# First weights in four pieces on ScalarE's queue, a later statistic, DeltaNet's side work one unit on, and norm spreads as rounded products

## The chip, the cores and the metric

The kernel runs on one core of one Trainium2 chip. The metric is the device time of one execution in microseconds, the median of several runs; the time before is 1535.09 us (three runs: 1535.09, 1535.09 and 1531.98).

## What is computed

A decoder trunk of two layers over 512 positions of width 1024, in float32:

```python
for layer in range(2):
    j = layer // 2
    if layer % 2 == 0:
        h = h + gated_deltanet(rms_norm(h, dn_norm[j]), ...)   # 8 heads of 128, chunked delta rule
    else:
        h = h + conformer_conv(rms_norm(h, cv_norm[j]), ...)   # GLU, causal conv of width 31, LayerNorm
    h = h + memory_cross_attention(rms_norm(h, xa_norm[layer]), rms_norm(mem, xa_mem_norm[layer]), ...)
    h = h + sq_relu_mlp(rms_norm(h, mlp_norm[layer]), ...)     # 1024 -> 4096 -> 1024
return rms_norm(h, final_norm)

def rms_norm(x, g):
    return x * lax.rsqrt(jnp.mean(x * x, axis=-1, keepdims=True) + 1e-6) * g
```

Gated DeltaNet projects h to q, k, v, z and to 16 gate columns (b and a per head), runs a causal convolution of width 4 over q, k and v, applies SiLU and a normalisation to q and k, and then carries a 128 x 128 state per head from chunk to chunk, with a decay made from the a column and a strength beta made from the b column.

## The kernel before

Activations lie transposed: a tile is 128 channels by 512 positions, and x is eight such tiles. Weights come from HBM as 128 x 1024 tiles of 512 KB ("units" of weights: one output tile of 128 channels with its eight blocks of 128 input channels). Every product is made of three rounded ones: a float32 operand is split into a rounded high part (fp32r) and the rounded rest, and high x high, low x high and high x low are summed in PSUM (`mm3`, lines 229 to 231). ScalarE casts the high part of a weight tile (`wh`, line 207), VectorE subtracts to get the low part (`wl`, line 70 by way of `wsplit`). Three weight tiles of each kind are in flight (NW = 3), three raw ones.

The RMS norm is not applied to the input of a projection. `Norm.parts` makes xh and xl of gain x h for each of the eight tiles (lines 297 and 73), and the projection of them is scaled behind the product by the reciprocal root of each position. That number is made by `Norm.stat`: the squares are summed over the eight tiles, four small products with a column of ones (ssq, line 315) sum over the channels, ScalarE takes the root, VectorE the reciprocal, and VectorE multiplies the identity with it into a diagonal `dg`. `Norm.spread` multiplies a 128 x 128 matrix of ones with dg in full float32 (line 325), which repeats the number over all 128 partitions, and ScalarE copies that to `rb`. There are six such norms (n0 of the DeltaNet, then the first attention, the first MLP, the conformer, the second attention and the second MLP); the memory has a spread of the same kind over 256 columns (`mem_diag`, `mem_spread`).

The DeltaNet stage is written as a list of main steps on TensorE (`mains`) and a table of side steps (`S.at(unit, rank, ...)`). `run` issues main step i and then the side steps of unit i. A unit of the q, k and v projections is half a head, 12 matmuls; z and the memory's K and V have units of 12 or 24. Unit 0 is `mm_ab`: head 0 of k together with the 16 gate columns (psum `ab`), 40 matmuls; units 1 to 3 have no main step. The constants at the end of the file place the side steps: T_STAT the statistic (the spread two units on, the gates three), T_DEC the decay (its sums `ct` two units before), K2 and Q2 the products among k and q, FS the forward substitution, MG the merging of its blocks, REC the recurrence of each group of four heads, ONORM the norm of its output, HO the transposes into the output projection (`ogT`), TAPV the convolution of v. The tile framework then orders the instructions of each engine from this list; what the order is can be read from the built program. `tc.keep_in_program_order` pins an instruction to its place in the list.

`gates` needs rb: it scales the gate columns, transposes them (abT, line 356), and makes beta, the log decay g and its repeated form `grep` in some twenty small VectorE operations. `decay_sums` multiplies grep (ct, line 419).

At the start SP's queue issues prm, wab (the gate columns' weights), raw0 (the first weight tile, one DMA) and the eight x tiles. TensorE first runs WARM = 13 products of ones.

Of the kernel before, what the change touches and what calls it, by code (L numbers as in the profile page):

```python
# [38 lines left out]
def tile_trunk(ctx, tc, xT, memT, prm_d, adt_d, bdw_d, tap_d, fin_d, w_ab, w_kq, w_v, w_z, w_dno, w_pw1, w_pw2,  # L39
               w_q, w_k, w_vv, w_o, w_up, w_dn, yT):  # L40
    nc = tc.nc
    pe, act, dve, pool = nc.tensor, nc.scalar, nc.vector, nc.gpsimd

    cp = ctx.enter_context(tc.tile_pool(name="cp", bufs=1))
    wp = ctx.enter_context(tc.tile_pool(name="wp", bufs=2))
    fsp = ctx.enter_context(tc.tile_pool(name="fsp", bufs=3))
    up = ctx.enter_context(tc.tile_pool(name="up", bufs=NSLOT))
    sp = ctx.enter_context(tc.tile_pool(name="sp", bufs=13))
# [8 lines left out]
    def slot(dt=F32, s="u", shape=(P, NT)):  # L57
        return up.tile(list(shape), dt, tag="u", name=nm(s))
# [10 lines left out]
    def tt(e, o, a, b, op):  # L69
        return e.tensor_tensor(out=o, in0=a, in1=b, op=op)  # L70

    def stt(o, a, s, b, op0, op1):
        dve.scalar_tensor_tensor(out=o, in0=a, scalar=s, in1=b, op0=op0, op1=op1)  # L73

    def ts(e, o, a, s1, op0, s2=None, op1=None):
        if op1 is None:
# [15 lines left out]
    def pc(name, i=0):  # L92
        return prm[:, OFF[name] + i:OFF[name] + i + 1]

    def load_x():
        r = []
        for t in range(KT):
            h = slot(s="x")
            nc.sync.dma_start(out=h, in_=xT[t * P:(t + 1) * P, :])
# [7 lines left out]
    nc.sync.dma_start(out=raw0, in_=w_kq[0][:, 0:1024])  # L107
# [19 lines left out]
    later = const([P, P], "later", F32R)  # L127
# [38 lines left out]
    for kind, gq in DN_ORDER:  # L166
        for i in range(2):
            j = gq * 2 + i
# [58 lines left out]
    def mm3(ps, wk, xk, first, last):  # L227
        (wh, wl), (xh, xl) = wk, xk
        pe.matmul(ps, wh, xh, start=first, stop=False)  # L229
        pe.matmul(ps, wh, xl, start=False, stop=False)  # L230
        pe.matmul(ps, wl, xh, start=False, stop=last)  # L231

    def wk(w, k):
        c = slice(k * P, (k + 1) * P)
        return w[0][:, c], w[1][:, c]
# [45 lines left out]
    class Sides(dict):  # L281
        def at(self, i, rank, f, *a):
            self.setdefault((i, rank), []).append(lambda: f(*a))


    class Norm:
        def __init__(self, gname, eng=None, deng=None):
            self.eng, self.deng = eng or pool, deng or dve
# [6 lines left out]
        def parts(self, t, h):  # L295
            xh = slot(F32R, "xh")
            act.activation(xh, h, AF.Copy, scale=pc(self.g, t))  # L297
            xl = slot(F32R, "xl")
            stt(xl, h, pc(self.g, t), xh.bitcast(F32), ALU.mult, ALU.subtract)
            self.xs.append((xh, xl))  # L300

        def square(self, h):
# [8 lines left out]
        def stat(self):  # L311
            ps = psum("ssq")
            for c in range(4):
                cs = slice(c * P, (c + 1) * P)
                pe.matmul(ps[:, c:c + 1], self.acc[:, cs], ones[:, 0:1], start=True, stop=True)
# [3 lines left out]
            dve.reciprocal(self.tok, sd)  # L319
            self.dg = slot(s="dg")  # L320
            tt(self.deng, c4(self.dg), over_c(ident), over_i(self.tok), ALU.mult)

        def spread(self):
            ps2 = psum("rb")
            pe.matmul(ps2, ones, self.dg, start=True, stop=True)
            self.rb = slot(s="rb")
            act.copy(self.rb, ps2)

# [439 lines left out]
            del mem[k]  # L768

    def mem_diag():  # L770
        mem["dg"] = slot(s="mdg")
        tt(dve, mem["dg"][:, 0:256].rearrange("p (t j) -> p t j", t=2), over_c(ident, 2), over_i(mem["tok"]), ALU.mult)

    def mem_spread():
        ps = psum("mrs")
        pe.matmul(ps[:, 0:256], ones, mem.pop("dg")[:, 0:256], start=True, stop=True)
        mem["rs"] = slot(s="mrs")
        act.copy(mem["rs"][:, 0:256], ps[:, 0:256])

# [485 lines left out]
    S.at(0, 3, wsplit)  # L1265
    S.at(0, 2, squares, SQ0, 8)
    S.at(T_STAT, 0, n0.stat)
    S.at(T_STAT + 2, 0, n0.spread)
    for h in range(8):
        uk = max(at["k", h] + 1, T_STAT + 2)  # L1270
# [7 lines left out]
    S.at(T_STAT + 3, 1, D.decay_const, 0)  # L1278
# [151 lines left out]
DEC1 = (37, 43)  # L1430
K2 = (14, 13, 16, 17, 43, 44, 47, 46)
Q2 = (16, 18, 20, 21, 46, 48, 48, 51)
FS = ((20, 9), (50, 8))
MG = (34, 67)
V2 = (8, 8)
MGAIN = 12
ONORM = (72, 87)
HO = 76
REC = (42, 74)
MEM = 50  # L1440
MSQ = 14
TAPV = (35, 36, 37, 38, 68, 68, 69, 70)
# [104 lines left out]
```

## Time and profile before

| | us |
|---|---|
| median of three runs | 1535.09 |
| the profiled execution's own time | 1534.16 |
| its span, first to last instruction | 1532.4 |
| TensorE busy | 1514.5 |
| VectorE busy | 895.2 |
| ScalarE busy | 678.8 |
| GpSimd busy | 221.6 |
| mean granted clock | 0.996 |

The profile is of one execution. Its page gives the busy time of each engine, and a line such as `PE ... x512 | 200.2, 391` means 512 instructions, 200.2 us busy together, 391 ns one. Matmuls overlap: one that is listed with 0.39 us follows the one before by 0.23, so what a matmul costs is read from the distance of starts. A product in full float32 appears as two instructions (x2). In a list of waits, `PE S L682 <- DVE vnd L70: 1.2, 1, 1.2` says that TensorE's product into S, line 682, waited for VectorE's vnd, 1.2 us in all, once, 1.2 us at most. In a timeline the columns are start, duration, engine, line, operation, result and operands, count; the brackets hold idle time before and what ended it.

### The profile page before, as it was taken

To read this page: it belongs to the slowest core of one execution; us is meant where nothing else is said; L and a number is where in the kernel's file an instruction comes from. 1 tells how busy PE (TensorE), PEld (TensorE's weight loads), DVE (VectorE), ACT (ScalarE), POOL (GpSimd) and SP (SyncE) were. 2 spreads that over 40 slices of the span, in tenths; PEclk is the share of its full clock that TensorE was granted. 3 is DMA by queue.
4 is the path that set the end of the run, shared out by engine and by line. 5 is a ranking of instruction groups with operands and counts; after the bars stand their busy time and mean duration, and the time that the engine had idled before them with its cause. 6 is when DMAs were issued, how large, how long until landed. Compare 5 with 4: busy or idle time off the path is not lost.

```text
span 1532.4 us, 19347 instructions
## 1 busy us (share of the span) xinstructions
PE 1514.5 (99%) x7560; PEld 1275.3 (83%) x7560; DVE 895.2 (58%) x1342; ACT 678.8 (44%) x1093; POOL 221.6 (14%) x231
## 2 busy tenths in 40 slices
PE   9999999999999999999999999999999999999998
PEld 7888888988888888888888889888888888888886
DVE  6898888766545443443445599774554543434441
ACT  6847655655434442332324564464444441323332
POOL 1321220103112000000002486411111000000000
PEclk9999999999999999999999999999999999999999
DMA  5321123342213222222224524442212222222231
GB/s 178 98 81 65 60 79 111 124 147 87 70 42 110 85 100 98 98 98 100 97 94 162 170 91 142 140 132 92 76 46 96 96 96 97 96 98 97 99 106 55
DMA packets 49051, 153.56 MB, mean 100 GB/s; under 512 B 6208, under 2 KB 8000, under 8 KB 48960
## 3 DMA queue, kind: packets, MB, share of 16 engines
q1 hardware_dynamic: 48960, 152.33, 29.8%
q8 instruction: 59, 0.97, 0.3%
q14 instruction: 32, 0.26, 0.1%
HBM read 149.42 MB, written 2.10 MB: 99 GB/s over the span
## 4 chain that ended last, share of the span: by engine, by line
PE 73%; DVE 5%; DMA 1%; SPq 1%; issue 1%; ACT 1%; POOL 0%; ACTq 0%; DVEq 0%
PE up L231 8%; PE up L229 8%; PE up L230 8%; PE dn L231 7%; PE dn L230 7%; PE dn L229 7%; DVE ca L73 3%; PE q L229 2%; PE xo L230 2%; PE q L231 2%; PE q L230 2%; PE xo L231 2%; PE xo L229 2%; PE pw L230 2%; PE pw L229 2%; PE pw L231 2%
## 5 line engine op out<-in xcount | busy, mean ns | idle before, releaser
L207 ACT CAST wh<-raw 128x1024 fp32r<-128x1024 f32 x248 | 259.9, 1050 | 627.7 <-PE dn L230 194.8
L70 DVE TENSOR_TENSOR wl<-raw,wh 128x1024 fp32r<-128x1024 f32 x231 | 286.3, 1241 | 110.4 <-ACT wh L207 109.2
L229 PE MATMUL up<-xh,wh 128*128 128x512 f32 x512 | 200.2, 391 | 0.0
L231 PE MATMUL up<-xh,wl 128*128 128x512 f32 x512 | 199.2, 389 | 0.0
L230 PE MATMUL up<-xl,wh 128*128 128x512 f32 x512 | 199.2, 389 | 0.0
L231 PE MATMUL dn<-uh,wl 128*128 128x512 f32 x448 | 174.3, 389 | 0.0
L229 PE MATMUL dn<-uh,wh 128*128 128x512 f32 x448 | 174.3, 389 | 0.0
L230 PE MATMUL dn<-ul,wh 128*128 128x512 f32 x448 | 174.3, 389 | 0.0
L70 DVE TENSOR_TENSOR h<-dn,h 128x512 f32<-128x512 f32 x56 | 41.8, 747 | 165.3 <-PE dn L231 165.3
L73 DVE SCALAR_TENSOR_TENSOR rl<-up,rb 128x512 f32<-128x512 f32 x64 | 44.2, 691 | 156.9 <-PE up L231 156.9
L70 POOL TENSOR_TENSOR sq<-sq,sq 128x512 f32<-128x512 f32 x30 | 48.3, 1610 | 469.2 <-ACT sq L304 469.2
L230 PEld LDWEIGHTS up<-xl,wh 128*128 128x128 f32 x512 | 96.1, 188 | 20.5 <-issue 0.5
L229 PEld LDWEIGHTS up<-xh,wh 128*128 128x128 f32 x512 | 96.1, 188 | 20.2 <-issue 0.5
L231 PEld LDWEIGHTS up<-xh,wl 128*128 128x128 f32 x512 | 96.1, 188 | 20.0
L230 PEld LDWEIGHTS dn<-ul,wh 128*128 128x128 f32 x448 | 84.1, 188 | 17.6
L229 PEld LDWEIGHTS dn<-uh,wh 128*128 128x128 f32 x448 | 84.1, 188 | 17.5
L231 PEld LDWEIGHTS dn<-uh,wl 128*128 128x128 f32 x448 | 84.1, 188 | 17.2
L73 DVE SCALAR_TENSOR_TENSOR ca<-x,prm,ca 128x512 f32<-128x512 f32 x112 | 82.3, 753 | 3.5 <-ACT ca L1070 1.3
L229 PE MATMUL h<-xh,wh 128*128 128x512 f32 x192 | 77.5, 404 | 1.4 <-ACT xh L297 1.4
L230 PE MATMUL h<-xl,wh 128*128 128x512 f32 x192 | 75.4, 393 | 0.6 <-DVE xl L73 0.6
L231 PE MATMUL h<-xh,wl 128*128 128x512 f32 x192 | 75.4, 393 | 0.0
L73 DVE SCALAR_TENSOR_TENSOR cva<-cv,prm,cva 128x512 f32<-128x512 f32 x60 | 49.4, 840 | 11.7 <-POOL cva L70 10.4
(346 smaller groups left out, 3065.1 us busy)
## 6 DMA issues: line engine op xcount, KB each, us to landing
raw<-w_up SPq DMA_DIRECT2D x64, 512.0 KB, 3.5
raw<-w_dn SPq DMA_DIRECT2D x64, 512.0 KB, 3.5
raw<-w_pw SPq DMA_DIRECT2D x24, 512.0 KB, 3.6
raw<-w_kq SPq DMA_DIRECT2D x16, 512.0 KB, 3.8
raw<-w_k SPq DMA_DIRECT2D x16, 512.0 KB, 4.1
raw<-w_vv SPq DMA_DIRECT2D x16, 512.0 KB, 3.6
raw<-w_q SPq DMA_DIRECT2D x16, 512.0 KB, 3.6
raw<-w_o SPq DMA_DIRECT2D x16, 512.0 KB, 3.6
```

What stands on the lines that cost most here:

```text
L70: return e.tensor_tensor(out=o, in0=a, in1=b, op=op)
L73: dve.scalar_tensor_tensor(out=o, in0=a, scalar=s, in1=b, op0=op0, op1=op1)
L207: ins = [act.copy(h, raw)]
L229: pe.matmul(ps, wh, xh, start=first, stop=False)
L230: pe.matmul(ps, wh, xl, start=False, stop=False)
L231: pe.matmul(ps, wl, xh, start=False, stop=last)
```

## The change

Four things at once. (1) The first weight tile is loaded by four DMAs of 256 columns issued from ScalarE's queue; on SP wab follows the first x. Casts and subtractions of the quarters and of the x tiles are pinned in the order in which the inputs arrive, two x for each quarter, with the gate weights' cast behind x 0. The second weight tile is split right behind them, ahead of the squares. `mm_ab` takes its products in the order high x high, low weight x high, gates, high weight x low, gates. (2) T_STAT goes from 2 to 5; the spread follows one unit later instead of two and the gates two units later instead of three, so that they stand at units 6 and 7 where they stood at 4 and 5. T_DEC and all other places of DeltaNet's side steps go up by one (MGAIN, MEM and MSQ stay). (3) All norms but n0 and the memory's norm split the reciprocal root into a rounded part and the rest, make two diagonals, and spread them by two rounded products; the matrix `later`, used up to then by the decay, is overwritten with ones for that. (4) WARM goes from 13 to 11.

```diff
-    def load_x():
+    def load_x(then=None):
...
             r.append(h)
+            if then and t == 0:
+                then()
...
     nc.sync.dma_start(out=prm[:, 0:NVEC], in_=prm_d[:, 0:NVEC])
+    raw0 = wp.tile([P, 1024], F32, tag="raw", name="raw0", bufs=NRAW)
+    for i in range(4):
+        act.dma_start(out=raw0[:, i * 256:(i + 1) * 256], in_=w_kq[0][:, i * 256:(i + 1) * 256])
     wab = slot(s="wab")[:, 0:P]
-    nc.sync.dma_start(out=wab, in_=w_ab)
-    raw0 = wp.tile([P, 1024], F32, tag="raw", name="raw0", bufs=NRAW)
-    nc.sync.dma_start(out=raw0, in_=w_kq[0][:, 0:1024])
-    xin = load_x()
+    xin = load_x(lambda: nc.sync.dma_start(out=wab, in_=w_ab))
...
+    def diag2(v, n):
+        vh = sp.tile([P, n], F32R, tag="sm", name=nm("vh"))
+        dve.tensor_copy(vh, v)
+        vl = small(n, "vl")
+        tt(dve, vl, v, vh.bitcast(F32), ALU.subtract)
+        r = []
+        for x in (vh.bitcast(F32), vl):
+            d = slot(F32R, "dg")[:, 0:n * P]
+            tt(dve, d.rearrange("p (c i) -> p c i", c=n), over_c(ident, n), over_i(x), ALU.mult)
+            r.append(d)
+        return r
+
+    def spread2(ps, dg):
+        for i in range(2):
+            pe.matmul(ps, later, dg[i], start=i == 0, stop=i == 1)
...
-            pe.matmul(ps2, ones, self.dg, start=True, stop=True)
+            if self.two:
+                spread2(ps2, self.dg)
+            else:
+                pe.matmul(ps2, ones, self.dg, start=True, stop=True)
...
     def mem_diag():
-        mem["dg"] = slot(s="mdg")
-        tt(dve, mem["dg"][:, 0:256].rearrange("p (t j) -> p t j", t=2), over_c(ident, 2), over_i(mem["tok"]), ALU.mult)
+        act.copy(later, ones)
+        mem["dg"] = diag2(mem["tok"], 2)
...
-    act.copy(ab3[:, :, 0:16], wab.rearrange("p (k x) -> p k x", k=KT))
-    tt(dve, ab3[:, :, 16:32], wab.rearrange("p (k x) -> p k x", k=KT), ab3[:, :, 0:16].bitcast(F32), ALU.subtract)
+    n0 = Norm("dn_norm", dve, False)
...
+    for i in range(4):
+        s = slice(i * 256, (i + 1) * 256)
+        pin(act.copy(hl0[0][:, s], raw0[:, s]))
+        pin(tt(dve, hl0[1][:, s], raw0[:, s], hl0[0][:, s].bitcast(F32), ALU.subtract))
+        for k in (2 * i, 2 * i + 1):
+            n0.parts(k, xin[k], pin)
+            if k == 0:
+                wab3 = wab.rearrange("p (k x) -> p k x", k=KT)
+                pin(act.copy(ab3[:, :, 0:16], wab3))
+                pin(tt(dve, ab3[:, :, 16:32], wab3, ab3[:, :, 0:16].bitcast(F32), ALU.subtract))
     wsplit()
-    n0 = Norm("dn_norm", eng=dve)
-    for t in range(KT):
-        n0.parts(t, xin[t])
...
-            mm3(D.ps["k", 0], wk(w, k), n0.xs[k], k == 0, k == KT - 1)
-            xh, xl = n0.xs[k]
+            (xh, xl), (wh, wl), ps = n0.xs[k], wk(w, k), D.ps["k", 0]
+            pe.matmul(ps, wh, xh, start=k == 0, stop=False)
+            pe.matmul(ps, wl, xh, start=False, stop=False)
             pe.matmul(D.ps["ab"][0:32, :], abp[:, 32 * k:32 * k + 32], xh, start=k == 0, stop=False)
+            pe.matmul(ps, wh, xl, start=False, stop=k == KT - 1)
...
-    S.at(T_STAT + 2, 0, n0.spread)
+    S.at(T_STAT + 1, 0, n0.spread)
...
-    S.at(T_STAT + 3, 0, D.gates)
+    S.at(T_STAT + 2, 0, D.gates)
...
-WARM = 13
+WARM = 11
...
-T_STAT = 2
-T_DEC = 12
+T_STAT = 5
+T_DEC = 13
...
-K2 = (14, 13, 16, 17, 43, 44, 47, 46)
+K2 = (15, 14, 17, 18, 44, 45, 48, 47)
...
-REC = (42, 74)
+REC = (43, 75)
...
```

More of the change, by code (lines that the diff above doesn't have):

```diff
@@ L72, in stt @@
     def stt(o, a, s, b, op0, op1):
-        dve.scalar_tensor_tensor(out=o, in0=a, scalar=s, in1=b, op0=op0, op1=op1)
+        return dve.scalar_tensor_tensor(out=o, in0=a, scalar=s, in1=b, op0=op0, op1=op1)
     def ts(e, o, a, s1, op0, s2=None, op1=None):
@@ L283, in at, with __init__ @@
             self.setdefault((i, rank), []).append(lambda: f(*a))
+    def diag2(v, n):
[12 more added lines that the diff above has]
+            pe.matmul(ps, later, dg[i], start=i == 0, stop=i == 1)
     class Norm:
[L287 to L288 removed]
+        def __init__(self, gname, eng=None, two=True):
+            self.eng, self.two = eng or pool, two
             self.g, self.acc, self.xs, self.n = gname, None, [], 0
@@ L293, in add, with parts @@
             self.square(h)
-        def parts(self, t, h):
+        def parts(self, t, h, pin=lambda i: i):
             xh = slot(F32R, "xh")
-            act.activation(xh, h, AF.Copy, scale=pc(self.g, t))
+            pin(act.activation(xh, h, AF.Copy, scale=pc(self.g, t)))
             xl = slot(F32R, "xl")
-            stt(xl, h, pc(self.g, t), xh.bitcast(F32), ALU.mult, ALU.subtract)
+            pin(stt(xl, h, pc(self.g, t), xh.bitcast(F32), ALU.mult, ALU.subtract))
             self.xs.append((xh, xl))
@@ L314, in stat @@
                 cs = slice(c * P, (c + 1) * P)
-                pe.matmul(ps[:, c:c + 1], self.acc[:, cs], ones[:, 0:1], start=True, stop=True)
+                ins = pe.matmul(ps[:, c:c + 1], self.acc[:, cs], ones[:, 0:1], start=True, stop=True)
+                if not self.two:
+                    tc.keep_in_program_order(ins)
             sd = small(4, "sd")
@@ L319, in stat @@
             dve.reciprocal(self.tok, sd)
+            if self.two:
+                self.dg = diag2(self.tok, 4)
+                return
             self.dg = slot(s="dg")
-            tt(self.deng, c4(self.dg), over_c(ident), over_i(self.tok), ALU.mult)
+            tt(dve, c4(self.dg), over_c(ident), over_i(self.tok), ALU.mult)
         def spread(self):
             ps2 = psum("rb")
-            pe.matmul(ps2, ones, self.dg, start=True, stop=True)
+            if self.two:
+                spread2(ps2, self.dg)
+            else:
+                pe.matmul(ps2, ones, self.dg, start=True, stop=True)
             self.rb = slot(s="rb")
@@ L770, in mem_diag @@
     def mem_diag():
-        mem["dg"] = slot(s="mdg")
-        tt(dve, mem["dg"][:, 0:256].rearrange("p (t j) -> p t j", t=2), over_c(ident, 2), over_i(mem["tok"]), ALU.mult)
+        act.copy(later, ones)
+        mem["dg"] = diag2(mem["tok"], 2)
     def mem_spread():
         ps = psum("mrs")
-        pe.matmul(ps[:, 0:256], ones, mem.pop("dg")[:, 0:256], start=True, stop=True)
+        spread2(ps[:, 0:256], mem.pop("dg"))
         mem["rs"] = slot(s="mrs")
```

24 lines of the change are left out of this document (14 added, 10 removed).

## The prediction, made before the changed kernel ran

> **What bounds the kernel now.** I read the page's shares first, then the list of TensorE's waits, then the timelines of the few places that the change touches.
>
> ```profile
> PE 1514.5 (99%) x7560; PEld 1275.3 (83%) x7560; DVE 895.2 (58%) x1342; ACT 678.8 (44%) x1093; POOL 221.6 (14%) x231
> ...
> L70 DVE TENSOR_TENSOR wl<-raw,wh 128x1024 fp32r<-128x1024 f32 x231 | 286.3, 1241 | 110.4 <-ACT wh L207 109.2
> ```
>
> ```profile
> PE K L231 <- DVE wl L70: 3.3, 2, 2.9
> PE vn L669 <- ACT cvq L459: 1.6, 1, 1.6
> PE h L229 <- ACT xh L297: 1.4, 1, 1.4
> PE S L682 <- DVE vnd L70: 1.2, 1, 1.2
> ...
> PE ai L506 <- ACT cva L466: 0.5, 1, 0.5
> PE dt L441 <- DVE L L73: 0.4, 1, 0.4
> PE vn L669 <- DVE r L73: 0.3, 1, 0.3
> ```
>
> TensorE (PE) is the bound from end to end: it is busy for 99% of the span, and its waits come to some 12 us in all. So time is gained in three ways only: matmul work taken out, waits taken out, or a slow clock avoided; and any new wait of PE is paid in full. The profiled execution took 1534.16 us, its span 1532.4, so 1.8 us lie around the span. The three runs have a median of 1535.09, 0.9 above it. Sums are made against 1534.16.
>
> The start shows all three:
>
> ```profile
> 0.80 1.28 ACT L126 ACT_TABLE_LOAD   x1 [0.80 <-PEq L1538]
> ...
> 1.20 5.85 PE L118 MATMUL warm<-ones 128*128 128x128 f32 x26 [1.20 <-POOL ones L115]
> ...
> 1.71 0.43 SPq L107 DMA_DIRECT2D raw<-w_kq  x1
> ...
> 2.09 0.30 ACT L126 CAST ident_r<-ident 128x128 fp32r<-128x128 f32 x1
> 2.18 4.90 SPq L99 DMA_DIRECT2D x<-xT  x8
> ...
> 6.76 1.04 ACT L207 CAST wh<-raw 128x1024 fp32r<-128x1024 f32 x1 [3.39 <-DMA raw<-w_kq]
> 7.71 5.17 ACT L297 ACTIVATE xh<-x,prm 128x512 fp32r<-128x512 f32 x8
> 8.48 0.49 PE L229 MATMUL h<-xh,wh 128*128 128x512 f32 x1 [1.43 <-ACT xh L297]
> 8.98 5.38 DVE L73 SCALAR_TENSOR_TENSOR xl<-x,prm,xh 128x512 fp32r<-128x512 f32 x8
> 20.21 0.95 PE L315 MATMUL ssq<-ones,sq 128*128 128x1 f32 x8
> ```
>
> The next rows are those of the busy time by stretch: stretch, its length, PE busy (count), PEld, DVE, ACT, POOL, granted clock, DMA share, GB/s.
>
> ```profile
> 6.85:10.26 3.41, 1.41 (x6) 0.61 (x5) 2.43 (x3) 3.41 (x6) 0.00 (x0) 1.00 1.05 403
> 10.26:13.67 3.41, 3.41 (x10) 2.24 (x8) 3.41 (x7) 3.41 (x7) 0.00 (x0) 0.50 1.02 348
> 13.67:17.08 3.41, 3.41 (x16) 2.25 (x16) 3.10 (x6) 3.41 (x8) 0.00 (x0) 1.00 0.49 198
> ...
> 979.60:986.40 6.80, 5.90 (x27) 5.90 (x28) 4.59 (x6) 1.02 (x2) 0.00 (x0) 0.50 0.68 233
> ```
>
> The thirteen warm-up matmuls end at 7.05, the weights land at 6.76, the first real matmul starts at 8.48. PE is then busy for 1.41 of 3.41 us, and the next 3.41 us are granted half the clock: 10 matmuls instead of 16, so 6 x 0.23 = 1.4 us lost. The same happens after the longest wait at 977. The first forty matmuls (head 0 and the gate columns) end where the statistic begins, at 20.21.
>
> **The change part by part.** *Start.* The first weights leave SP's queue for ScalarE's, as four DMAs of 128 KB; on SP x 0 is now second and wab third. ScalarE issues four times at SP's 0.47 each (1.71 to 2.18), from 0.80 to 2.7; behind them stand its table load and the ident_r cast (1.28 + 0.30, to 4.3), then the first quarter's cast. How early x 0 lands no row shows. In these rows the landing of x and of wab is given from the issue:
>
> ```profile
> x<-xT SPq DMA_DIRECT2D x8, 256.0 KB, 5.7
> ...
> wab<-w_ab SPq DMA_DIRECT2D x1, 64.0 KB, 1.8
> ```
>
> From below: second in its queue as wab is now, one issue (0.47) after SP's first at 0.80, 1.27 + 1.8, and 0.65 us for 256 KB at the 403 GB/s of the stretch from 6.85: 3.7. From above: as late as now, where its cast starts at 7.71: 7.5. With all four quarters (512 KB, 1.3 us) ahead of it: 5.0. I take 5.0, because only one DMA stands before it on its own queue. Its cast takes 0.71 (by 8.48 less 7.71, with the hand-over), so xh 0 is there at 5.7, and the warm-up decides: eleven at 0.45 (5.85/13) end at 1.20 + 4.95 = 6.15. PE starts at 6.2 (8.2 at worst). SP's remaining issues wait, in the built program, for the eighth transfer before them over both queues; x 2 thus waits for the first quarter, x 4 for the second, and the next weights for x 2 as they do now.
>
> From there PE must be fed. A pair of x with its quarter costs ScalarE 2 x 0.65 + 0.41 = 1.7 us (0.41 lies on the line from 0.30 at 128 columns to 1.04 at 1024), VectorE 2 x 0.67 + 0.42 = 1.8; PE needs 10 x 0.23 = 2.3 for them. So PE is the slower one and runs on: 0.65 us at half clock (1.5 matmuls), 38.5 x 0.23 = 8.9, about 0.4 for the first subtract and the gate cast: end at 16.1 against 20.21, **-4.1** (from -4.5 to -0.3). The second head's weights follow x 7 on SP's queue with prm's rest (134 + 512 KB, 1.6 us at 403 GB/s); x 7 is cast at 12.2 now (7.71 + 7 x 0.65), so they land by 14 at the latest. Their cast (1.04) now stands before the squares, and with the subtract of 1.24 they are ready near 16.4, when PE's third product there needs them (16.1 + 0.5). Eight squares behind it, at the casts' 0.65 or less, end by 20.3, the sums by 21.0, ahead of the statistic at 21.6, which now has 24 more matmuls before it.
>
> *Gates.* The statistic moves three units on, the spread two, the gates two, but the decay only one. In the built program the gates' transposes are followed by 48 matmuls up to the decay sums (ct), now 60:
>
> ```profile
> 27.68 0.43 PE L356 MATMUL abT<-ident,ab 32*128 32x32 f32 x4
> 33.83 0.69 DVE L70 TENSOR_TENSOR cv<-h,rb 128x512 f32<-128x512 f32 x1 [1.78 <-PE h L231]
> 34.43 0.17 DVE L77 TENSOR_SCALAR sm<-sm 128x32 f32<-128x32 f32 x1
> 38.38 0.19 DVE L73 SCALAR_TENSOR_TENSOR sm<-sm,sm 128x32 f32<-128x32 f32 x1
> 39.13 0.16 DVE L396 COPY grep<-g 128x128 f32<-128x128 f32 x1
> 41.79 0.38 PE L419 MATMUL ct<-tri_mid,grep 128*128 128x128 f32 x2
> ```
>
> Now grep is done 2.5 us before ct. After, VectorE's queue holds the eviction of the last of those 48 (cv of q 0) in front of the last six gate operations. ct stands right behind that head on PE, so PE must wait for one eviction, 0.60 (33.83 to 34.43), and for 38.38 to 39.29, 0.91, with 0.15 of hand-over: **+1.65**. The gate work before it fills VectorE until about the same moment, so up to 1 more. The transposes wait for two evictions put before the gate product: **+0.3**. Behind ct seven matmuls instead of four stand before the dt product that waits 0.4 now: **-0.4**.
>
> *Spreads.* Five norms (not the first) and the memory's spread two rounded products instead of one in full precision:
>
> ```profile
> 835.81 0.23 PE dn L231
> ...
> 854.66 0.86 PE rb L325 x2
> ```
>
> ```profile
> 850.55 0.69 DVE L70 TENSOR_TENSOR dg<-ident,rstd 128x512 f32<-128x512 f32 x1
> ```
>
> 0.86 - 2 x 0.23 = 0.40 each, five times 2.0, and half that for the memory's 256 columns: **-2.2**. VectorE does a copy, a subtract (0.17 each by the row at 34.43) and a second 0.69 more, 1.05 per norm; dg is ready at 851.2 and used at 854.66, so 2.4 us of cover remain. Without that cover it would be the 1.05 each.
>
> *One unit on.* All of DeltaNet's side work keeps its distances but stands one unit (12 matmuls, 2.7 us) later against the projections. Neither order nor trace gives the waits of the two recurrences; they are 1.6, 1.2, 0.5 and 0.3 now. In the built order the second recurrence's state product (1.2) has 24 V matmuls before it where 12 of the out projection stood, so it loses most of its wait; the first one's vn keeps 12 matmuls and nearly the same VectorE queue. I take **-1.0**; bounds are all four gone, -3.6, and each of the four longer by the whole unit of 2.7 (+10.8). At the end of the recurrence the unit is missing:
>
> ```profile
> 341.40 0.89 PE o L699 x8
> ...
> 353.03 1.91 PE L732 MATMUL ogT<-ident,z 128*128 128x128 f32 x16
> ```
>
> ```profile
> 345.67 0.24 DVE L723 RECIPROCAL sm<-sm 128x16 f32<-128x16 f32 x1
> ...
> 345.99 3.54 POOL L70 TENSOR_TENSOR z<-z,sm 128x512 f32<-128x512 f32 x3 [53.30 <-DVE sm L723]
> 347.56 1.06 ACT L207 CAST wh<-raw 128x1024 fp32r<-128x1024 f32 x1 [2.07 <-PE do L230]
> ```
>
> The last o ends at 342.3, ogT runs 48 matmuls later. After, 36 (8.2 us) are left, and ScalarE's root stands behind a weight cast that waits for the first 12 of them (2.75) and takes 1.06; VectorE's reciprocal stands behind that cast's subtract (1.24). Reciprocal near 5.1 + 0.24 and GpSimd's 3.54: 8.95 after o, against 8.2: **+0.9** with what follows (0 to 2).
>
> Sum: -4.1 + 1.65 + 0.3 - 0.4 - 2.2 - 1.0 + 0.9 = -4.85, hence 1529.3. The wait at 977 and its half clock stay: the conformer's queues keep their order.
>
> **The rivals.** *(B) The quarters bring nothing*, because all transfers run at the same 400 GB/s already (403 in the stretch 6.85:10.26) and x 0 waits in the crowd. For it: an x lands 5.7 us after its issue. Against: wab's 1.8, and 512 KB stood before x 0 on one queue. PE then starts at 8.2, the clock drops as now, the start gains 0.3 instead of 4.1: 1533.1. The Trainium skill says just this ("DMA: Bandwidth & Descriptors", section "Issuing engines are not separate DMA queues"): several issuers save the time of issuing alone. By that rule only the place in the queue can help.
>
> *(C) The clock.* PE starts early, yet one stretch of 3.41 us more is granted half clock, because the shorter warm-up or the crumbs of waits among the first products leave a stretch too idle (1.41 of 3.41 was). It costs 1.4: 1530.7. The Trainium skill ("TensorE: Matmul & The Clock Gate", Part 1, the HAM clock gate) has the window free-running, not restarted by a kernel; by that rule the place of the stretches changes from run to run, and 1.4 may come or go in either kernel.
>
> *(D) Slower.* VectorE, busy 184 of 210 us between 30 and 240,
>
> ```profile
> 30.00:240.00 210.00, 207.59 (x1190) 178.05 (x1189) 184.45 (x380) 131.64 (x237) 47.60 (x94) 1.00 0.24 78
> ```
>
> cannot give the unit back: what ct shows (a queue entry tied to a later head) is repeated at the four waits of the recurrences, each time for the whole unit: +10.8 in place of -1.0, 1541.1. It decides once these waits exceed today's by 3.85 us (the sum without its -1.0). Against it: the waits now are only 3.6 in that stage, and the distances among the moved pieces stay.
>
> *(E) All four waits vanish*, 2.6 more: 1526.7.
>
> **How the numbers follow.** Forecast (A) 0.57, C 0.14, B 0.13, D 0.08, E 0.08. About 0.2% (3 us) is what a measurement can tell from no change; against the median that is below 1532.0 for faster and above 1538.2 for slower. A, C and E lie below (0.79); A's own range of 1526.5 to 1532.5 passes that edge, so I give 0.75; same has B and what A and C lose, 0.17; slower is D, 0.08. The range 1525.3 to 1533.4 holds A, C, E and B, and leaves out D.
>
> **What would show it.** First matmul at 6.2 and the statistic's column sums at about 21.6 behind 24 extra matmuls (gain at the end of the forty: 4.1); granted clock 1.00 from about 7 on; a wait of ct on grep of 1.6; spreads of 0.46; ogT waiting 0.7 for GpSimd's z; the list of waits without S. I am wrong if x 0 lands after 5.4, if PE's stretch before 14 is granted 0.50, or if the recurrences' waits add up to more than 3.6.

## The result, and the profile after

| | before | after |
|---|---|---|
| median | 1532.38 (7 runs, 1530.72 to 1535.09) | 1537.72 (7 runs, 1536.53 to 1540.29) |
| ratio, 95% interval | | 1.0033 (1.0023 to 1.0043) |
| profiled execution's span | 1532.4 | 1535.9 |
| TensorE busy | 1514.5 | 1512.7 |

The three runs of before that stand at the head of this document are the first of the seven here. The change made the kernel 5.3 us slower by the medians, where 4.85 less were forecast. The forecast started from one execution of 1534.16, 1.8 above the median of the seven; that moves its time, but not its difference. One run of e13 below took 2162.69 us, and every other run of this document lies within 0.5% of the median of its kernel.

The start did what it should. The list of TensorE's waits of the changed kernel shows where the time went; its columns are the sum, the number of times and the longest, in us.

```profile
PE K L233 <- DVE wl L70: 4.9, 2, 2.6
PE mg L620 <- ACT w L610: 1.8, 1, 1.8
PE ct L446 <- DVE grep L423: 1.7, 1, 1.7
PE vt L648 <- ACT cva L493: 1.7, 1, 1.7
PE vn L696 <- DVE r L73: 1.7, 1, 1.7
...
PE dt L468 <- DVE L L73: 1.1, 1, 1.1
...
PE S L709 <- DVE vnd L70: 0.4, 1, 0.4
...
PE ogT L759 <- POOL z L70: 0.3, 1, 0.3
...
PE abT L383 <- DVE ab L70: 0.2, 1, 0.2
PE rb L352 <- DVE dg L70: 0.2, 1, 0.2
```

`mg`, which never waited before, waits 1.8 us; `vt` waits 1.7 in the first half of the heads, where it did not wait (its 0.3 of before was in the second half), `dt` 1.1 instead of 0.4; of K's 4.9, 2.3 belong to the memory's K inside DeltaNet (0.4 before). `vn` waits as long as before, but for another tile (r, on VectorE, instead of cvq, on ScalarE). S fell from 1.2 to 0.4, `ct` has the 1.7 that was forecast. All waits together are 17.3 us instead of 12.1; with 1.8 us less of busy time that is, to 0.1, the 3.5 us by which the span of the profiled execution grew. The start and two places in the stage, as rows of TensorE's timeline and of the busy time by stretch (columns as in the prediction):

```profile
5.67 0.50 PE L1277 MATMUL h<-xh,wh 128*128 128x512 f32 x1 [0.34 <-ACT xh L316]
...
21.37 0.83 PE L334 MATMUL ssq<-ones,sq 128*128 128x1 f32 x6
```

```profile
4.19:7.60 3.41, 2.82 (x16) 1.89 (x16) 1.75 (x4) 2.43 (x7) 1.37 (x3) 1.00 1.06 374
...
79.30:82.70 3.40, 3.32 (x23) 2.73 (x23) 3.15 (x9) 3.30 (x7) 1.25 (x5) 1.00 0.40 148
82.70:86.10 3.40, 3.40 (x10) 2.66 (x9) 1.90 (x3) 3.30 (x7) 1.17 (x4) 0.50 0.25 81
205.60:209.00 3.40, 3.25 (x28) 2.86 (x26) 3.31 (x11) 2.06 (x5) 1.56 (x4) 1.00 0.45 159
209.00:212.40 3.40, 3.40 (x9) 2.71 (x9) 3.14 (x7) 1.72 (x3) 1.62 (x3) 0.50 0.30 77
```

The first real matmul starts at 5.67 (8.48 before), the granted clock is 1.00 from 4.19, and with 24 matmuls (5.5 us) between the forty and the sums at 21.37 the forty end at 15.9: 4.3 us sooner. Behind that TensorE gives the lead back. The two last pairs of rows are two new stretches of 3.4 us that ran at half clock, which costs at most 1.7 us each; but over all runs the mean granted clock is 0.997 in both kernels, so on average they only stand for the stretches at 10.26 and 979 that went or became shorter.

What the list of waits does not show is the reason for `mg`. These are ScalarE's rows of before between 40 and 65 us, table loads and the decay's exponentials (`egd`, `dt`) alone:

```profile
42.49 1.28 ACT L466 ACT_TABLE_LOAD   x1
...
49.32 1.28 ACT L437 ACT_TABLE_LOAD   x1
50.62 0.25 ACT L437 ACTIVATE egd<-gsum 128x96 f32<-128x96 f32 x1
...
52.01 2.22 ACT L443 ACTIVATE dt<-dt 128x512 f32<-128x512 f32 x4
...
54.74 1.28 ACT L466 ACT_TABLE_LOAD   x1
```

and those of after:

```profile
45.91 1.28 ACT L493 ACT_TABLE_LOAD   x1
...
50.55 1.28 ACT L464 ACT_TABLE_LOAD   x1
51.84 0.25 ACT L464 ACTIVATE egd<-gsum 128x96 f32<-128x96 f32 x1
52.11 1.28 ACT L493 ACT_TABLE_LOAD   x1
...
54.05 1.28 ACT L470 ACT_TABLE_LOAD   x1
55.35 1.08 ACT L470 ACTIVATE dt<-dt 128x512 f32<-128x512 f32 x2
...
58.48 1.09 ACT L470 ACTIVATE dt<-dt 128x512 f32<-128x512 f32 x2
...
61.51 1.28 ACT L493 ACT_TABLE_LOAD   x1
```

L466 (now L493) is the silu of k and q. Before, one silu phase ends, all exponentials run, the next silu phase begins. After, a silu stands between `egd` and the first `dt`: ScalarE loads its table twice more, 2.6 us. Between 20 and 130 us it loads 10 times instead of 8. From 130 to 370 it loads 7 times instead of 9, so that the number for the whole stage is 17 in both kernels: what hurts is where the two loads stand. Behind `dt` hangs the longest chain of the stage: decay blocks, their transpose (FT), 31 dependent rounds of substitution on VectorE, the transpose of their result (TB), then `w` on ScalarE and `mg` on TensorE. In VectorE's rows FT and TB are

```profile
81.20 1.23 DVE L540 STREAM_TRANSPOSE FT<-DB 128x1024 f32<-128x1024 f32 x1
...
114.92 2.11 DVE L556 STREAM_TRANSPOSE TB<-X 128x1024 f32<-128x1024 f32 x1
```

before, and after

```profile
86.16 1.25 DVE L567 STREAM_TRANSPOSE FT<-DB 128x1024 f32<-128x1024 f32 x1 [1.44 <-ACT DB L560]
...
122.58 2.11 DVE L583 STREAM_TRANSPOSE TB<-X 128x1024 f32<-128x1024 f32 x1
```

VectorE, with 31 rounds ahead of it, waits for ScalarE, and TB comes 7.7 us later. One unit is 2.7, and the projections had come 4.3 sooner. The delay grows along the chain: `egd` is 1.2 later, the first `dt` 3.3, FT 5.0, TB 7.7.

### The profile page after: what moved, and what is told of

Same layout as the page of the kernel before. It is cut to its first block, busy times and chain, and to the rows that moved or that the text cites. A ratio compares the mean times of both kernels' runs of the same rounds, so it can differ in the third digit from the quotient of the medians.

```text
span 1535.9 us, 19365 instructions
## 1 busy us (share of the span) xinstructions
PE 1512.7 (98%) x7556; PEld 1273.1 (83%) x7556; DVE 897.9 (58%) x1363; ACT 677.5 (44%) x1097; POOL 221.5 (14%) x231
## 4 chain that ended last, share of the span: by engine, by line
PE 69%; DVE 6%; ACT 1%; issue 1%; POOL 0%; ACTq 0%; DVEq 0%; POOLq 0%
PE up L231 8%; PE up L232 8%; PE up L233 8%; PE dn L232 7%; PE dn L231 7%; PE dn L233 7%; DVE ca L73 4%; PE q L231 2%; PE xo L232 2%; PE xo L233 2%; PE q L233 2%; PE q L232 2%; PE xo L231 2%; PE pw L232 2%; PE pw L231 2%; PE pw L233 2%
## 5 line engine op out<-in xcount | busy, mean ns | idle before, releaser
L70 DVE TENSOR_TENSOR wl<-raw,wh 128x1024 fp32r<-128x1024 f32 (+1 forms) x234 | 287.6, 1231 | 106.7 <-ACT wh L209 100.5
L70 DVE TENSOR_TENSOR h<-dn,h 128x512 f32<-128x512 f32 x56 | 41.8, 747 | 165.3 <-PE dn L233 165.3
L70 POOL TENSOR_TENSOR sq<-sq,sq 128x512 f32<-128x512 f32 x30 | 48.3, 1610 | 464.3 <-ACT sq L323 454.5
L231 PE MATMUL h<-xh,wh 128*128 128x512 f32 x184 | 73.3, 398 | 0.0
L232 PE MATMUL h<-xl,wh 128*128 128x512 f32 x184 | 72.1, 392 | 0.0
L233 PE MATMUL h<-xh,wl 128*128 128x512 f32 x184 | 71.8, 390 | 0.0
L73 DVE SCALAR_TENSOR_TENSOR cva<-cv,prm,cva 128x512 f32<-128x512 f32 x60 | 46.2, 795 | 11.0 <-POOL cva L70 10.5
```

The source lines that it names most:

```text
L73: return dve.scalar_tensor_tensor(out=o, in0=a, scalar=s, in1=b, op0=op0, op1=op1)
```

## The experiments

Medians are in us; runs of one group share their runs of before. First each part of the change alone, or alone undone.

**e1, the spreads alone.** The new spreads in the kernel before.

> The kernel before, with only the five norm spreads and the memory's spread in two rounded products. Theory T1 (the unit by which DeltaNet's side work stands later makes VectorE and ScalarE late for TensorE, and that alone lost the time) and theory T2 (the late statistic lost it) both expect the forecast's term: -2.2 us (ratio 0.9986), each spread 2 x 0.23 instead of 0.86, no new wait of TensorE on dg. Theory T3 (the spreads themselves cost time, by VectorE's extra 1.05 us per norm) expects 0 to +3 us, with a wait of rb on dg.

1531.37 on 1533.29 (the median of this kernel on that of before), ratio 0.9986 (95% interval 0.9977 to 0.9995): -1.9. The forecast's -2.2 holds for this part by itself.

**e2, the unit alone.**

```diff
-T_DEC = 12
+T_DEC = 13
...
-REC = (42, 74)
+REC = (43, 75)
```

> The kernel before, with only the constants that put DeltaNet's decay, transposes, recurrences and output norm one unit later; start, statistic and spreads as before. T1: slower by 5 to 9 us (ratio 1.003 to 1.006), with new waits at mg, at cva before vt, and longer ones of a wl product in DeltaNet, as the changed kernel has. T2: within 2 us of before, since the statistic is early and the distances among the moved pieces stay. T4 (only the two stretches at half clock, at 82.7 and 209, lost the time, and they come by chance): within 2 us, and such stretches at other places or none.

1539.11 on 1533.29, 1.0044 (1.0030 to 1.0057): +5.8 by the medians, 6.7 by the ratio. Waits: vt 2.5, vn 1.5, S 1.6, K's wl product at 267 2.0; TB at 120.4; 10 table loads. (The profile is that of the slowest of the five runs, 1544.48.) So the unit costs by itself what had been forecast as a gain of 1.0.

**e3, the unit undone.** The changed kernel with the unit's constants as before; T_STAT and WARM stay changed.

> The changed kernel with those constants put back to the kernel before; the early start, the late statistic (three units on) and the new spreads stay. T1: the loss in DeltaNet goes but for ct and dt, so -4.3 (start) -2.2 (spreads) +2.5 (ct, dt, abT) = 4 us faster than before (ratio 0.9974). T2: as slow as the changed kernel or slower, 3 to 8 us above before (ratio 1.002 to 1.005), because the decay now stands one unit nearer to the late gates: ct waits 1.7 + 2.7 = 4.4 us.

1534.83, 1.0010 (1.0001 to 1.0019). Neither theory: without the unit the kernel is 2.9 faster, but the start and the spreads, worth 6.2 together, bring nothing: it is 1.5 slower than before. `mg` waits 1.8 here too, the products of sqq (squares of q, line 547) wait 1.1, and there are 10 table loads.

**e4, the start with the early statistic.** T_STAT = 2, gates, unit and spreads as before.

> The changed kernel's start alone: quarters on ScalarE's queue, eleven warm-ups, pinned casts; statistic, gates, unit and spreads as in the kernel before. The forty matmuls end at 16 again, 4.3 us sooner, but the squares end at about 20.3 and the statistic's column sums stand right behind the forty: T2 and T1 both expect a wait of TensorE on sq there of about 4 us, and so no gain (-1 to +1 us; ratio 0.9993 to 1.0007). If the squares are done sooner than I think, 4.3 us faster (0.9972), and then the statistic need not have been moved at all.

1539.03, 1.0039 (1.0026 to 1.0052). The statistic waits 5.6 us for the squares (`PE ssq L334 <- DVE sq L70`), and 10.2 us, begun inside that wait, run at half clock (18.3 to 28.5). Table loads 8, no wait at `mg`: the late statistic is needed, and it brings the loads (e3 has 10 with the unit undone). The unit brings them too, without it (e2).

Second group, on e3: is the statistic's chain or VectorE the limit?

**e5, the statistic sooner.**

```diff
+        for t in range(4):
+            sq = slot(s="sq")
+            tt(pool, sq, xin[t], xin[t], ALU.mult)
...
-        for t in range(t0, t1):
+        for t in range(4, t1):
             n0.square(xin[t])
-T_STAT = 5
+T_STAT = 4
```

> The changed kernel with the unit undone (as e3), and in addition: GpSimd squares and sums x 0 to 3, ScalarE and VectorE only x 4 to 7, so that the squares are done some 2.5 us sooner, and the statistic, its spread and the gates stand one unit (12 matmuls) sooner. Theory T5 (the statistic cannot come sooner, so the lead of 4.3 us that TensorE gains at the start is given back to the chain statistic, gates, decay, substitution, merge, at ct, dt, sqq and mg): ct's 1.7, mg's 1.8 and most of dt's 0.8 and sqq's 1.1 go, 4 to 5 us less than e3, so about 1530 (ratio 0.998). Rival T6 (VectorE has no room in 30 to 130 whatever its input's time): the waits only move on, within 1.5 us of e3 (1533.3 to 1536).

1537.59 on 1533.23, 1.0032 (1.0019 to 1.0045); both were wrong, for GpSimd's work slows VectorE's here. VectorE's rows while GpSimd squares:

```profile
8.10 1.52 DVE L73 SCALAR_TENSOR_TENSOR xl<-x,prm,xh 128x512 fp32r<-128x512 f32 x1
9.55 1.51 DVE L70 TENSOR_TENSOR wl<-raw,wh 128x256 fp32r<-128x256 f32 x1
```

and GpSimd's:

```profile
9.04 1.74 POOL L70 TENSOR_TENSOR sq<-sq,sq 128x512 f32<-128x512 f32 x1
10.74 1.22 POOL L70 TENSOR_TENSOR sq<-x 128x512 f32<-128x512 f32 x1
```

The same two VectorE operations take 0.74 and 0.41 in the changed kernel, where GpSimd rests: the two engines seem to take turns, and the start loses what the statistic was to gain. This agrees with the Trainium skill ("SBUF — State Buffer", section "SBUF: two separate sides"): the two engines hold one pair of ports in turn, for a whole instruction. Still, `ct` waits only 0.2 here while sqq (1.3) and `mg` (1.9) stay: these two do not come from late gates alone (there are 10 table loads here as well).

**e6, ct one unit later.** `S.at(T_DEC - 1, 2, D.decay_sums)`.

> The kernel of e3 with the decay sums (ct) one unit later, behind 12 more matmuls. If ct's wait of 1.7 is only a place badly chosen, it goes and nothing follows: -1.7 us against e3. T5 and T6 (VectorE's chain behind ct is late anyway) expect the wait to move on to dt: ct 0, dt 0.8 to 2.5 or more, and within 0.7 us of e3, or slower, since the substitution starts later still and mg waits longer than 1.8.

1534.62, 1.0010 (1.0001 to 1.0020). The framework left ct where it was on TensorE, so this is e3 once more (0.2 apart) and tells nothing of ct.

**e7, mg one unit later.** `MG = (35, 67)` on e3.

> The kernel of e3 with only the first half's merge (mg) one unit later. T5: mg's wait of 1.8 goes, its successors (vt, vn) have the slack that they have in the kernel before, so 1 to 1.8 us below e3. T6: vt or vn then wait as they do in the changed kernel (1.7 each), and the time stays within 0.7 us of e3 or rises.

1536.03, 1.0017 (1.0008 to 1.0026): `mg`'s wait falls to 0.6 in two places, but 0.6 comes at its next step, 1.1 at a `dt` at 153, and it is 1.2 slower than e3. This place for `mg` does not take the late chain out of TensorE's way.

**e8, the second part of the unit alone,** on the kernel before (the lines put in):

```diff
+MG = (35, 68)
+V2 = (9, 9)
+ONORM = (73, 88)
+HO = 77
+REC = (43, 75)
+TAPV = (36, 37, 38, 39, 69, 69, 70, 71)
```

> The kernel before with only the second part of the unit: merge, value transposes, recurrences and output norm one unit later; decay, k and q transposes and the substitution where they were. The whole unit cost 6.7 us alone (e2), with waits at vt 2.5, vn 1.5, S 1.6, a wl product at 267 2.0. If these come from the recurrences' own place, this part alone costs 4 to 7 us. If they come from the late substitution and decay before them, this part costs 0 to 2 us.

1531.70, 0.9990 (0.9981 to 0.9999): -1.5. `vn` of the first half no longer waits (1.6 before), and S of the second half waits 0.4 instead of 1.2. The forecast's -1.0 for these pieces has the right size, in part by luck: S lost its wait as argued, but `vn`, which lost most, was to keep it. The loss is in the other pieces: decay, k and q products, substitution.

The table loads between 20 and 130 us are 8 in before, e1, e4 and e8, and 10 in after, e2, e3, e5, e6 and e7. Third group:

**e9, the loads taken out of the changed kernel.**

```diff
-T_DEC = 13
+T_DEC = 12
-    S.at(T_DEC + 1, 2, D.decay, [2, 3])
+    S.at(T_DEC, 2, D.decay, [2, 3])
-LAG = (0, 0, 1)
+LAG = (0, 1, 1)
```

> The changed kernel with three small shifts: all four heads of the first decay in one unit, one unit sooner (as in the kernel before), and the silu of q one unit later. ScalarE then loads its table 8 times between 20 and 130 us as in the kernel before, instead of 10. Theory T7 (two more table loads of 1.28 us on ScalarE, between the decay's exponentials and the silus, delay dt, the blocks DB, the substitution and so mg by 2.6 us, and that is most of what the late statistic and the unit lost): sqq's and mg's waits (1.1 and 1.8) go, ct's 1.7 stays, and the second part of the unit brings its 1.5: 3 to 6 us below the changed kernel, so 1532 to 1535 on its 1537.7 (ratio to before 0.999 to 1.001). Rival T8 (the late gates alone make the chain late, whatever ScalarE loads): within 1.5 us of the changed kernel (ratio 1.002 to 1.004), mg waits 1.5 or more.

1537.55 on 1533.18, 1.0024 (1.0015 to 1.0034): a miss for T7 by the time, 4.4 above before where the changed kernel had 5.3, and a miss for T8 by the waits. `mg` waits only 0.5 instead of 1.8 and `vn` 0.9 instead of 1.7, but S of the first half now waits 2.0, `vt` 2.2 instead of 1.7, and K's wl keeps its 2.3. So the loads are not all of it.

**e10, the decay one unit later still.** `T_DEC = 14`.

> The changed kernel with only the first decay one unit later still. The table is loaded 8 times there too, but the decay stands 2.7 us later. T7: ct's wait goes, the two loads saved (2.6) and the later place (2.7) cancel at mg, so mg still waits 1 to 2.5 us: 1 to 3 us below the changed kernel (ratio to before 1.0005 to 1.003). T8: ct's wait goes and mg's grows by 2.7: the same as the changed kernel or slower (1.003 to 1.006).

1535.37, 1.0011 (1.0002 to 1.0019), as T7 has it by the time, 8 loads; but `mg` waits only 0.6, and vt 2.2, vn 1.5 and K 2.3 remain.

**e11, loads added to the kernel before.**

```diff
                 act.activation(self.egd, ps_g[:, 0:96], AF.Exp)
+                act.activation(small(1), eps_rms, AF.Silu)
```

(with `egd`, this and the first `dt` pinned).

> The kernel before with one silu of a 128x1 tile put between the decay's exponentials. With what the order of the built program makes of it, ScalarE loads its table 12 times in that stage instead of 8: 5.1 us more on ScalarE, and nothing else is added. T7: the substitution starts 3 to 5 us later, TensorE waits at dt, sqq and mg as in e3, and the time rises by 3 to 6 us (ratio 1.002 to 1.004). If ScalarE had the room (it is busy 44% of the span), the time stays within 1 us.

1539.87, 1.0045 (1.0031 to 1.0058): +6.7. 12 loads; FT at 90.3, TB at 125.6; sqq waits 2.5 and `mg` 0.9 and 0.8. ScalarE, busy 44% of the span, has no room in this stage. What the three pins cost without the silu was not measured.

**e12, the two parts that gained, together.** e1 and e8.

> The kernel before with the two parts that gained alone: the rounded spreads (e1, -1.9) and the second part of the unit (e8, -1.5); the start as before. If the two add up: -3.4 us, about 1529.8 (ratio 0.9978). If they share a cover (VectorE before the recurrences), between -1.9 and -3.4.

1534.80, 1.0007 (0.9999 to 1.0016): not -3.4 but +1.6. TensorE's rows show a wait that neither had:

```profile
258.17 0.28 PE L231 MATMUL K<-mh,wl 128*128 128x256 f32 x1
261.02 0.38 PE L229 MATMUL K<-mh,wh 128*128 128x256 f32 x1 [2.57 <-ACT wh L207]
...
262.28 0.58 PE L231 MATMUL K<-mh,wl 128*128 128x256 f32 x1 [0.76 <-DVE wl L70]
```

The granted clock halves behind it (261.7 to 265.1), and its mean over the runs is 0.9954, where e1 and e8 have 0.997: by estimate (0.0016 of the span) 2.5 us, of which not all need come from this stretch. Two things were open: this wait, and which part makes vt, S and K wait in e9.

**e13 and e14, a pair.** The changed kernel with the first part of the unit undone, the second kept. e14 is just that; in e13 the silu of q 0 is one unit later and the first decay in one unit.

> The changed kernel with the first part of the unit undone (decay, k and q transposes, substitution where the kernel before has them), the second part kept, all four heads of the first decay in one unit and the silu of q 0 one unit later, so that ScalarE loads its table 8 times in the stage. T7 (loads) with the first part as the source of the waits at vt, S and wl: ct 1.7 stays, sqq, mg, vt, S and wl under 0.6 each; 1.5 to 3 us below e14, 1529.5 to 1532 (ratio 0.9975 to 0.999). If the early start and the late statistic make those waits: they stay near 2 us each, 1534 to 1537.

> The same without the shift of the silu and of half the decay: 10 loads. T7: sqq waits 1.1, and the substitution ends 2 to 3 us later than in e13; 1532.5 to 1534.5 (ratio 0.9995 to 1.001). If loads do not matter: as e13.

e13: 1534.16 on 1532.31, 1.0011 (1.0002 to 1.0020), 8 loads. e14: 1537.63, 1.0041 (1.0029 to 1.0054), 10 loads. The difference is 3.5 us, more than T7's 1.5 to 3. ScalarE's rows, e13:

```profile
52.14 1.28 ACT L470 ACT_TABLE_LOAD   x1
53.43 2.07 ACT L470 ACTIVATE dt<-dt 128x512 f32<-128x512 f32 x4
```

e14:

```profile
51.52 1.28 ACT L470 ACT_TABLE_LOAD   x1
52.82 0.60 ACT L470 ACTIVATE dt<-dt 128x512 f32<-128x512 f32 x1
53.43 1.28 ACT L493 ACT_TABLE_LOAD   x1
...
55.38 1.28 ACT L470 ACT_TABLE_LOAD   x1
56.67 1.58 ACT L470 ACTIVATE dt<-dt 128x512 f32<-128x512 f32 x3
```

The last `dt` ends at 55.5 and 58.25, though e14 reached this place 0.6 sooner; TB comes at 116.8 and 120.8. That half of the decay stands one unit later in e14 is not the reason: TensorE has all four `dt` products done by 52.7 there, before ScalarE's first `dt`. e14's sqq wait of 1.1 and a `dt` wait of 1.1 at 151 are not in e13. vt (0.7 and 0.4) and S (0.4) are small in both: their long waits belong to the first part of the unit, and not, as the rival had it, to the early start and the late statistic, which both kernels have. But K waits 2.6 for wh in both, and both are slower than I expected by about that and its half clock, so that e13's time lies where the rival put it.

**e15, the gates sooner.** e13 with the gates at T_STAT + 1.

> e13 with the gates in the unit of the spread, one unit sooner: their operations then stand in front of the evictions on VectorE, and ScalarE loads its table once less (7). If ct's wait belongs to the place of the gates behind those evictions: ct under 0.3, for up to 0.8 at abT; 0.5 to 1.5 us below e13. If VectorE is simply full there, dt takes over ct's wait and the time is as e13.

1535.43, 1.0018 (1.0008 to 1.0027): `ct` no longer waits, 7 loads, and yet 1.3 above e13, with sqq waiting 1.6 and `dt` 1.0 at 148. `ct`'s wait, worked out rightly, buys nothing by going: other waits take its place.

**e16, the first part of the unit alone,** on the kernel before: T_DEC, DEC1, K2, Q2 and FS one up.

> The kernel before with the first part of the unit alone: first and second decay, k and q transposes, substitution one unit later; merge, recurrences and output norm where they were. The unit cost 6.7 (e2) and its second part brought 1.5 (e8), so 5 to 9 us slower (ratio 1.003 to 1.006), with 10 table loads in the stage and waits at mg of 2 us or more, since the merge is not moved.

1537.36, 1.0034 (1.0022 to 1.0046): +5.1, 10 loads, and 13 instead of 9 between 130 and 370; `mg` waits 1.8, K for wh 1.1 and for wl 0.8, TB at 119.3. e8 and e16 add up to 3.6, e2 had 5.8 to 6.7: the parts are not independent.

**e17 and e18, the memory's spread left as it was,** on e12 and on e13:

```diff
     def mem_diag():
-        act.copy(later, ones)
-        mem["dg"] = diag2(mem["tok"], 2)
+        mem["dg"] = slot(s="mdg")
+        tt(dve, mem["dg"][:, 0:256].rearrange("p (t j) -> p t j", t=2), over_c(ident, 2), over_i(mem["tok"]), ALU.mult)
...
     def mem_spread():
+        act.copy(later, ones)
...
-        spread2(ps[:, 0:256], mem.pop("dg"))
+        pe.matmul(ps[:, 0:256], ones, mem.pop("dg")[:, 0:256], start=True, stop=True)
```

The copy of ones into `later` moves with this edit, from `mem_diag` to `mem_spread`; in the traces of e12 and e17 it runs at 177.5 and takes 0.29 in both, so it has no part in the difference.

> e12 (the kernel before, rounded spreads, second part of the unit) with the memory's spread left in full precision; the five norms keep the rounded one. If VectorE's extra work for the memory's spread makes the second substitution late and K wait for wh: that wait falls from 2.6 to under 0.5, and the two gains add up, -3.4 us + 0.2, about 1529.5 (ratio 0.998). If the second part of the unit and the norms' spreads collide by themselves: the wait stays and the time is as e12 (1.0007).

> e13 (changed start, late statistic, second part of the unit, 8 table loads, rounded spreads) with the memory's spread left in full precision. By the same reason the wait for wh at 262 goes: 2 to 4 us below e13, 1530 to 1532 (ratio 0.9985 to 1), so the start, with what its late statistic costs at ct, dt and ai (about 3), is worth 0 to 1 us more or less than the old start of e17. Else as e13 (1.0011).

e17: 1529.40 on 1533.19, 0.9975 (0.9966 to 0.9984). e18: 1528.76, 0.9972 (0.9963 to 0.9981). Both beat the kernel before and the changed one, and the wait for wh is gone in both (K waits 0.5 for wl). VectorE's rows at the end of the second substitution, e12:

```profile
247.30 0.69 DVE L70 TENSOR_TENSOR cv<-h,rb 128x512 f32<-128x512 f32 x1 [0.81 <-PE h L231]
...
248.20 1.23 DVE L70 TENSOR_TENSOR wl<-raw,wh 128x1024 fp32r<-128x1024 f32 x1
...
249.78 2.09 DVE L579 STREAM_TRANSPOSE TB<-X 128x1024 f32<-128x1024 f32 x1
```

and ScalarE's:

```profile
253.09 6.81 ACT L596 COPY u<-UB 32x128 f32<-32x128 f32 x16 [4.92 <-DVE UB L579]
259.93 2.94 ACT L207 CAST wh<-raw 128x1024 fp32r<-128x1024 f32 x3
```

In e17:

```profile
246.15 2.10 DVE L579 STREAM_TRANSPOSE TB<-X 128x1024 f32<-128x1024 f32 x1
...
254.09 0.69 DVE L70 TENSOR_TENSOR cv<-h,rb 128x512 f32<-128x512 f32 x1
```

```profile
249.47 6.95 ACT L596 COPY u<-UB 32x128 f32<-32x128 f32 x16 [1.63 <-DVE UB L579]
256.45 2.00 ACT L207 CAST wh<-raw 128x1024 fp32r<-128x1024 f32 x2
```

The three more VectorE operations of the rounded spread take 1 us, but with them the built order puts an eviction (cv) and a weight subtract (wl) in front of the transposes where e17 has them behind: VectorE waits 0.8 for TensorE, then works 1.9 on these, and TB is 3.6 late. The 16 copies of u follow it on ScalarE, the weight cast follows them, and K waits. The memory's K is a neighbour that the change does not move.

## Why the prediction was wrong, step by step

Two steps failed, by about as much each. The unit by itself cost 5.8 us (e2) where -1.0 and +0.9 make -0.1; all the rest by itself cost 1.5 (e3) where the terms make -4.75. The two misses, 5.9 and 6.3, add up to more than the whole of 10.2, so the parts are not independent.

**The start, -4.1:** right as a place in time, wrong as a gain. First matmul 5.67 (forecast 6.2; eleven warm-ups end at 5.34, so that xh 0 decided, and not the warm-up), clock 1.00 from 4.19, the forty end at 15.9 (16.1). The step that failed is to book this as time saved, on the ground that TensorE is the bound from end to end: it was only a lead over the chain statistic, gates, decay, substitution. e18 against e17 says what it is worth in the end, with the late statistic and the two shifts that save the loads: 0.6 us, within the intervals.

**Gates, +1.65 and +0.3:** `ct` right, at 1.69, by the mechanism named (cv of q 0 in front of the last six gate operations). The transposes wait 0.16, and the spread another 0.16 for its diagonal, which was not forecast. **dt, -0.4:** wrong. I counted the matmuls ahead of it and not VectorE's queue: it waits 1.1.

**Spreads, -2.2:** right alone (-1.9, e1; the pair's second product follows 0.23 behind the first). The cover was argued for the five norms, with 2.4 us to spare, and carried over to the memory's spread without a row: there it took 5.4 us from e12 (e17), because of the order that it changed.

**"One unit on", -1.0 with bounds of -3.6 and +10.8:** this is the other step that failed, and its +5.8 is within its bounds only because they were so wide. Its sentence "All of DeltaNet's side work keeps its distances" was the mistake, twice. The silus of k and q and the evictions hang on the projections (the first of k on the spread) and did not move with it, so the decay's exponentials slid in among them: two more table loads, in e16 as in e2. The late statistic alone brings two as well (e3, e14), and it is those that e13 and e14 price at 3.5 us. And the second substitution moved one unit toward the memory's K, which stays (K waits 2.0 in e2, 0.5 in e8, where the substitution is not moved). The list of four recurrence waits, on which the term and both bounds were built, was the wrong list: these gained (e8, from 3.6 to 1.4 with the wait of kS that came new), while mg, vt, dt and K, which waited 0.3 to 0.4 or not at all, lost. The order of ScalarE's instructions in the built program shows the extra loads; I had read TensorE's and VectorE's.

**ogT, +0.9:** 0.3, by the mechanism named: the root stands behind the weight cast (355.6), the reciprocal behind its subtract, and z is done 8.6 after o.

**The rivals.** The sign was D's, with 0.08. Its place and its price were wrong: VectorE could give the unit back at the four recurrence waits. There the waits fell from 3.6 to 2.5 (vn 1.7, S 0.4, kS 0.4), so its condition was never met, and neither was any of the three signs of being wrong; a rival with the waits at the unmoved neighbours was missing. B, C and E did not happen: the start ran at full clock, and the half clock at 82.7 and 209 is not C's. The lower edge of the range, 1525.3, has no sum; it played no part.

**How far the causes are shown.** e18 is the changed kernel with three things taken back: the first part of the unit, two table loads and the memory's rounded spread. It is 4.4 us faster than before, where the changed kernel is 5.3 slower, so the loss lies in these three. That it comes near the forecast's 4.85 is luck: 3.8 of it are the spreads and the second part of the unit (e17). One by one, that two loads cost 3.5 us is shown on e14's base, that four cost 6.7 on before's, pins included; that the memory's spread costs 5.4 on e12's and e13's, half clock included. In the changed kernel as it is, taking the loads out alone changed little (e9, 1.0 against its own runs of before), because the waits at vt, S and K remained. Which of decay, k and q products and substitution makes vt and S wait was not tried, nor was the changed kernel with only the memory's spread put back.

## What to carry to other kernels

A faster start of the bounding engine is a lead, not a gain: before it is booked, find the chain of the other engines that it must meet, and ask whether that chain starts sooner too. When a list of side work is moved, look for what is not moved with it (an eviction, a silu, the next stage's weights), and read the built order of every engine; look in it for ScalarE's table loads, each 1.28 us here, that stand on a chain the bounding engine waits for. Try the parts of a bundle alone and then in pairs: here two gains of 1.9 and 1.5 came out 1.6 slower together, at the edge of the interval, and 3.8 faster once one small part was taken out.

## What had not been expected of the hardware

Each table load is 1.28 us with no idle time in front. The Trainium skill ("ScalarE: Activation LUTs", section "What ACT_TABLE_LOAD costs") gives the same load and a drain of about 1.4 us beside it; the rows here, where `egd` ends at 52.09 and the load starts at 52.11, show no such drain. The Trainium skill's rule to group calls by set (the same page, section "Table sets: the hidden batching unit") is what the change broke between 20 and 130 us.

Half clock was granted from 82.7 and from 209.0 though TensorE was busy 3.32 and 3.25 of the 3.4 us before. In each of these stretches sixteen matmuls are column sums (128x1), 1.8 and 1.7 us long together. Without them some 1.5 us of work is left, close to the 1.41 that stood before the half clock of the start, while stretches of the changed kernel in which TensorE was busy 1.74 (from 161.2) and 1.76 (from 185.1) were followed by full clock. In e14 the same reckoning leaves 1.4 from 68.2, with half clock behind, and 1.7 from 201.3, with full clock. So column sums may count as idle here; that fits these figures, and no run tested it. And runs of one kernel lie up to 5 us apart, the slower ones mostly with a lower mean granted clock: the changed kernel's span was 1534.8 at 0.999, and 1535.9 and 1538.5 both at 0.996.
